# A 256-token decoder layer on one core: the LRU's gates as fp32r halves, its softplus moved, its input in four banks, and memory's sums moved

## The chip, the cores and the metric

The kernel runs on one core of a Trainium2 chip. The metric is the device time of one execution in microseconds; the figure for the kernel before is the median of three runs. Engines are named as the profile names them: PE (TensorE; PEld is its weight load), DVE (VectorE), ACT (ScalarE), POOL (GpSimd) and SP (SyncE, which issues most DMAs).

## What is computed

One layer of an autoregressive decoder on 256 tokens of width 2048, in float32. The normalised input goes through one projection `w_in` whose columns are split among three groups of heads; the part that the change touches is the first group, the RG-LRU (512 channels, four diagonal blocks of 128), and the normalisations.

```python
h = rms_norm(x, mix_norm_g)
p = h @ w_in                       # split: lru_x, lru_z, ml_u, ml_o, ml_z, ml_i, ml_f, mo_q, mo_k, mo_v, mo_z
# group A, RG-LRU
xc = causal_conv(lru_x, conv_w, conv_b)              # four taps
r = sigmoid(block_diag(xc, wa) + ba)
i = sigmoid(block_diag(xc, wx) + bx)
log_a = -8.0 * r * softplus(-lam)
a = exp(log_a)
u = sqrt(-expm1(2.0 * log_a)) * (i * xc)
h_t = a_t * h_(t-1) + u_t
y_lru = h * silu(lru_z)
# group B: mLSTM on ml_*; group C: block attention on mo_*
x = x + concat(y_lru, y_ml, y_mo) @ w_out
# cross-attention into 256 memory tokens
x = x + memory_cross_attention(rms_norm(x, xa_norm_g), rms_norm(mem, mem_norm_g), xa_wq, xa_wkv, xa_wo)
out = rms_norm(x, final_norm_g)
```

## The kernel before

**Chunks.** All weight matrices are cut on the host into one stream `ws` of 512 KB chunks (some are smaller) in the order of the table `GROUPS`: lx (the LRU's input, 8 chunks), u0, u2, u4 (4 each), lz0 (4), o0 and o1 (8 each), lz2, q, k, z, v, out0 to out3, and then the cross-attention's. A chunk is loaded to a tile `raw` (4 buffers), copied by ACT to `wh`, its value rounded to fp32r, and DVE writes the remainder `wl` = raw - wh (6 buffers of each; `split`, lines 182 to 211: the copy is line 204, the subtraction goes through the helper `tt` of line 150). The activations are split in the same way (`a_x`, with the high and the low half side by side). A product is then three fp32r products: high by high, high by low, low by high.

**Matmuls.** `mm` issues the matmuls of a chunk. Groups of kind "C" (weights stationary, lines 267 and 268) use one 512-wide matmul for high by (high, low) and one 256-wide for low by high; their accumulators are two PSUM banks, one for each 128 columns, and whoever takes them out adds the two halves of the bank (`add_halves`, line 466). Kind "W", which only lx has, uses three 256-wide matmuls into half a bank (lines 274 to 281), so four blocks of columns fit two banks and need no addition. Kind "X" has the activations stationary (lines 289 to 291). Accumulators come from a pool of 4 banks, all other PSUM tiles from a second pool of 4 (`ps`).

**The order.** The program's order is the order of issue: every engine takes its instructions in order. The main loop goes over the chunks i. In each turn it splits up to chunk i + 4, issues the matmuls of chunk i, and lets `step` advance one piece of the background queue `bg` by one `yield`. When the last chunk of a group is done, `done` appends the work that has become possible.

**The LRU.** When lx is done, `lru_evac` copies it out; `stats("x")` (line 429) turns the sums of squares of x into the root mean square of each token (`rstd_x` on DVE and POOL), forms diagonal matrices `d_x` of it (line 447) and, two turns later, multiplies them by ones on PE (line 453), so that each token's factor stands in a row in all partitions (`rrow`); `lru_scale` multiplies on POOL. `softplus_lam` (line 389) works on 128 x 4 numbers in a chain of small DVE instructions and one Exp on ACT. `lru_core` runs the convolution, block by block: ACT the first tap, DVE three multiply-adds (line 510), one block in a turn; then the gates, two blocks in a turn: two fp32 matmuls with the weights `lw` and two sigmoids on ACT for each block (lines 516 to 519); then exponentials, the square root and the scan.

```python
bg(idle(2), stats("x"), lru_scale(), u_scale(), call(softplus_lam), lru_core())
```

**Memory.** While PE works on out2 and out3, `mem_stats` loads the memory, squares it on ACT, sums on POOL, and `stats("m")` sums over the partitions on PE (line 438), forms `d_m` and multiplies it on PE (line 453). It stands in the queue behind the four loads of x for the residual (`x1_load`), each of which takes a turn.

Of the kernel before, what the change touches and what calls it, by code (L numbers as in the profile page):

```python
# [39 lines left out]
def _t(off, *tiles):  # L40
# [4 lines left out]
    ("lx", "w_in", "W", "x", _cols(*_t(O_LX, 0, 1, 2, 3))),  # L45
# [61 lines left out]
def kernel(ctx: ExitStack, tc: tile.TileContext, xT, memT, x, mem, ws, vec_d, lw_d, fg_d, out):  # L107
# [144 lines left out]
    def mm(i):  # L252
# [3 lines left out]
        if j == 0:  # L256
            acc[g] = [accp.tile([128, 512], F32, tag="acc", name=f"acc_{name}{b}") for b in range(2)]
        a = acc[g]
        for kk in range(kc):
# [3 lines left out]
            if kind == "C":  # L263
                both = act_all[act][k // 2][:, k % 2, :, :].rearrange("p a b -> p (a b)")
                for m in range(2):
                    sl = slice(kk * n + m * 128, kk * n + m * 128 + 128)
                    P.matmul(a[m], h[:, sl], both, start=first, stop=False, skip_group_check=True)  # L267
                    P.matmul(a[m][:, :256], l[:, sl], xh, start=False, stop=last, skip_group_check=True)  # L268
            elif kind == "W":
                mv_h, mv_l = xh, xl  # L270
                for m in range(n // 128):
                    o = a[m // 2][:, (m % 2) * 256:(m % 2) * 256 + 256]
                    sl = slice(kk * n + m * 128, kk * n + m * 128 + 128)
                    P.matmul(o, h[:, sl], mv_h, start=first and m % 2 == 0, stop=False, skip_group_check=True)
                    P.matmul(o, h[:, sl], mv_l, start=False, stop=False, skip_group_check=True)
                    if i:
                        P.matmul(o, l[:, sl], mv_h, start=False, stop=last, skip_group_check=True)
                for m in range(n // 128 if i == 0 else 0):
                    o = a[m // 2][:, (m % 2) * 256:(m % 2) * 256 + 256]
                    sl = slice(kk * n + m * 128, kk * n + m * 128 + 128)  # L280
                    P.matmul(o, l[:, sl], mv_h, start=False, stop=False, skip_group_check=True)
# [57 lines left out]
    def expand(name, blk):  # L339
        t = bdp.tile([128, 6, 128], F32, name=f"bd_{name}", tag="bd")  # L340
        bd[name] = t
        for c in range(6):
            G.tensor_tensor(t[:, c, :].rearrange("p (b o) -> p b o", o=4), dmask,
                            blk(c)[:, None, :].to_broadcast([128, 32, 4]), OP.mult)

# [83 lines left out]
    def stats(which):  # L429
# [19 lines left out]
        if which == "x":  # L449
            yield  # L450
# [39 lines left out]
    def lru_evac(a):  # L490
# [3 lines left out]
        for b in range(2):  # L494
            S.activation(xp[:, 2 * b:2 * b + 2, 3:259], bank(a, b), AF.Copy)
# [8 lines left out]

    def lru_core():
        xp = L["xp"]
        xc = big(2, 4, 256)
        for c in range(4):
# [775 lines left out]
```

## Time and profile before

| | |
|---|---|
| runs | 518.6, 518.79, 519.13 us (median 518.79) |
| the profiled execution | 518.12 us, of which its span is 516.4 us |
| PE busy | 506.7 us (98%) |
| DVE busy | 345.4 us (67%) |
| ACT busy | 301.2 us (58%) |
| POOL busy | 60.3 us (12%) |
| HBM | 190 GB/s over the span |

The span runs from the program's first instruction to its last; the remaining 1.7 us of the profiled execution lie around it. Times in rows are counted from the span's start. An instruction's duration reaches from its start to its modelled end; on PE and, less so, on ACT and DVE the next instruction starts before that, so a cost is best read from the difference of two starts. "[idle before <-X]" is how long the engine sat idle before the row, and what ended that.

### The profile page before, as it was taken

To read this page: it belongs to the slowest core of one execution; us is meant where nothing else is said; L and a number is where in the kernel's file an instruction comes from. 1 tells how busy PE (TensorE), PEld (TensorE's weight loads), DVE (VectorE), ACT (ScalarE), POOL (GpSimd) and SP (SyncE) were. 2 spreads that over 40 slices of the span, in tenths; PEclk is the share of its full clock that TensorE was granted. 3 is DMA by queue.
4 is the path that set the end of the run, shared out by engine and by line. 5 is a ranking of instruction groups with operands and counts; after the bars stand their busy time and mean duration, and the time that the engine had idled before them with its cause. 6 is when DMAs were issued, how large, how long until landed. Compare 5 with 4: busy or idle time off the path is not lost.

```text
span 516.4 us, 7502 instructions
## 1 busy us (share of the span) xinstructions
PE 506.7 (98%) x2746; PEld 444.1 (86%) x2746; DVE 345.4 (67%) x558; ACT 301.2 (58%) x498; POOL 60.3 (12%) x76
## 2 busy tenths in 40 slices
PE   9999999999999999999999999999999999999994
PEld 7998889988888888889988888888888788888883
DVE  6758955797478755747745567654767857748774
ACT  6685677679563533353545756544558567748444
POOL 1804112000151111002000000000141111000000
PEclk9999999999999999999999999999999999999997
DMA  8996454567645545436743365578594555643704
GB/s 293 400 343 238 133 163 128 154 204 235 214 148 168 174 164 163 149 96 212 241 160 124 130 205 175 183 251 324 191 332 124 190 176 165 197 169 96 265 7 162
DMA packets 31508, 98.73 MB, mean 191 GB/s; under 512 B 3568, under 2 KB 4720, under 8 KB 31472
## 3 DMA queue, kind: packets, MB, share of 16 engines
q1 hardware_dynamic: 30896, 97.59, 56.6%
q10 hardware_dynamic: 576, 0.66, 0.4%
q8 instruction: 21, 0.34, 0.3%
q14 instruction: 15, 0.12, 0.1%
HBM read 96.15 MB, written 2.10 MB: 190 GB/s over the span
## 4 chain that ended last, share of the span: by engine, by line
PE 86%; DVE 4%; ACT 3%; issue 2%; DMA 2%; POOL 1%; SPq 0%; ACTq 0%; DVEq 0%; POOLq 0%
PE acc_out L291 5%; PE acc_out L289 5%; PE acc_out L290 5%; PE acc_u L267 4%; PE acc_k L267 4%; PE acc_q L267 4%; PE acc_z L291 4%; PE acc_z L289 4%; PE acc_z L290 4%; PE acc_cq L267 3%; PE acc_ck L267 3%; PE acc_q L268 2%; PE acc_u L268 2%; PE acc_k L268 2%; PE acc_v L291 2%
## 5 line engine op out<-in xcount | busy, mean ns | idle before, releaser
L150 DVE TENSOR_TENSOR wl<-raw,wh 128x1024 fp32r<-128x1024 f32 (+4 forms) x169 | 199.8, 1197 | 95.6 <-ACT wh L204 93.2
L204 ACT ACTIVATE wh<-raw 128x1024 fp32r<-128x1024 f32 (+2 forms) x160 | 158.8, 1013 | 35.7 <-DMA raw<-ws 12.3
L289 PE MATMUL acc_out<-wh,a_y 128*128 128x512 f32 x128 | 50.8, 397 | 0.0
L291 PE MATMUL acc_out<-wh,a_y 128*128 128x512 f32 x128 | 50.0, 390 | 0.0
L290 PE MATMUL acc_out<-wl,a_y 128*128 128x512 f32 x128 | 49.8, 389 | 0.0
L289 PE MATMUL acc_z<-wh,a_x 128*128 128x512 f32 x96 | 39.6, 413 | 0.0
L291 PE MATMUL acc_z<-wh,a_x 128*128 128x512 f32 x96 | 37.6, 392 | 0.0
L290 PE MATMUL acc_z<-wl,a_x 128*128 128x512 f32 x96 | 37.5, 390 | 0.0
L267 PE MATMUL acc_k<-a_x,wh 128*128 128x512 f32 x96 | 34.4, 402 | 0.0
L267 PE MATMUL acc_q<-a_x,wh 128*128 128x512 f32 x96 | 34.3, 399 | 0.0
L267 PE MATMUL acc_u<-a_x,wh 128*128 128x512 f32 x96 | 34.0, 399 | 0.0
L474 POOL TENSOR_TENSOR w<-ev,rrow 128x512 f32<-128x512 f32 x10 | 16.9, 1691 | 133.3 <-DVE ev L150 120.5
L291 PEld LDWEIGHTS acc_out<-wh,a_y 128*128 128x128 f32 x128 | 24.0, 188 | 5.1
L290 PEld LDWEIGHTS acc_out<-wl,a_y 128*128 128x128 f32 x128 | 24.1, 188 | 4.7
L289 PEld LDWEIGHTS acc_out<-wh,a_y 128*128 128x128 f32 x128 | 24.0, 188 | 4.6
L268 PE MATMUL acc_u<-a_x,wl 128*128 128x256 f32 x96 | 27.0, 281 | 0.0
L268 PE MATMUL acc_q<-a_x,wl 128*128 128x256 f32 x96 | 26.9, 280 | 0.0
L268 PE MATMUL acc_k<-a_x,wl 128*128 128x256 f32 x96 | 26.8, 279 | 0.0
L414 POOL TENSOR_TENSOR mask<-mask,yt 128x512 f32<-128x512 f32 x7 | 9.8, 1397 | 145.8 <-ACT yt L413 145.8
L267 PE MATMUL acc_lz<-a_x,wh 128*128 128x512 f32 x64 | 23.4, 406 | 0.0
L267 PE MATMUL acc_ck<-a_m,wh 128*128 128x512 f32 x64 | 22.9, 401 | 0.0
L267 PE MATMUL acc_cq<-a_h,wh 128*128 128x512 f32 x64 | 22.7, 399 | 0.0
(325 smaller groups left out, 1171.8 us busy)
## 6 DMA issues: line engine op xcount, KB each, us to landing
raw<-ws SPq DMA_DIRECT2D x138, 512.0 KB, 3.7
raw<-ws SPq DMA_DIRECT2D x24, 384.0 KB, 3.1
w<-x SPq DMA_DIRECT2D x8, 512.0 KB, 6.3
raw<-ws SPq DMA_DIRECT2D x8, 392.0 KB, 3.3
w<-memT SPq DMA_DIRECT2D x8, 256.0 KB, 3.7
w<-xT SPq DMA_DIRECT2D x7, 256.0 KB, 5.2
out<-xg SPq DMA_DIRECT2D x5, 256.0 KB, 2.9
w<-fg SPq DMA_DIRECT2D x2, 512.0 KB, 5.6
```

Source lines behind the costliest of these rows:

```text
L150: V.tensor_tensor(out, a, b, op)
L204: S.activation(h[:, :kc * n], r[:, :kc * n], AF.Copy)
L267: P.matmul(a[m], h[:, sl], both, start=first, stop=False, skip_group_check=True)
L268: P.matmul(a[m][:, :256], l[:, sl], xh, start=False, stop=last, skip_group_check=True)
L289: P.matmul(o, xh[:, sl], mh, start=first, stop=False)
L290: P.matmul(o, xh[:, sl], ml, start=False, stop=False)
L291: P.matmul(o, xl[:, sl], mh, start=False, stop=last)
L414: G.tensor_tensor(sq[which], sq[which], q, OP.add)
L474: G.tensor_tensor(dst, e, rb(which), OP.mult)
```

## The change

1. lx becomes a group of kind "C": four PSUM banks, one for each block of 128 columns, all of the accumulators' pool; u0, the next group, takes two banks of the other pool. `lru_evac` adds the two halves of each bank, as other groups do. For chunk 0 the low matmuls still stand behind all high ones.
2. The gates' matmuls work on fp32r halves: `lw_halves` splits the gates' weights (after chunk 11), `lru_core` splits each block of the convolution's result (ACT copies, DVE subtracts), and each gate takes three fp32r matmuls for one fp32. The four new tiles come from the activations' pool.
3. `softplus_lam` leaves the queue and is issued in turn 9 of the main loop, before that turn's square of x.
4. The four loads of x take two turns for four, `mem_stats` waits one turn more behind its last square, and `stats("m")` leaves two turns between its diagonal matrices and their matmuls, as `stats("x")` does.

```diff
@@ -42,7 +42,7 @@
 
 
 GROUPS = [
-    ("lx", "w_in", "W", "x", _cols(*_t(O_LX, 0, 1, 2, 3))),
+    ("lx", "w_in", "C", "x", _cols(*_t(O_LX, 0, 1, 2, 3))),
     ("u0", "w_in", "C", "x", _cols(*_t(O_U, 0, 1))),
     ("u2", "w_in", "C", "x", _cols(*_t(O_U, 2, 3))),
     ("u4", "w_in", "C", "x", _cols(*_t(O_U, 4, 5))),
@@ -254,7 +254,12 @@
         name, mat, kind, act, cols = GROUPS[g]
         h, l = hi_w.pop(i), lo_w.pop(i)
         if j == 0:
-            acc[g] = [accp.tile([128, 512], F32, tag="acc", name=f"acc_{name}{b}") for b in range(2)]
+
+            if name == "u0":
+                acc[g] = [ps(), ps()]
+            else:
+                acc[g] = [accp.tile([128, 512], F32, tag="acc", name=f"acc_{name}{b}")
+                          for b in range(4 if name == "lx" else 2)]
         a = acc[g]
         for kk in range(kc):
             k = kc * j + kk
@@ -262,23 +267,21 @@
             first, last = k == 0, k == NK - 1
             if kind == "C":
                 both = act_all[act][k // 2][:, k % 2, :, :].rearrange("p a b -> p (a b)")
-                for m in range(2):
-                    sl = slice(kk * n + m * 128, kk * n + m * 128 + 128)
-                    P.matmul(a[m], h[:, sl], both, start=first, stop=False, skip_group_check=True)
-                    P.matmul(a[m][:, :256], l[:, sl], xh, start=False, stop=last, skip_group_check=True)
-            elif kind == "W":
-                mv_h, mv_l = xh, xl
+
+                def high(m):
+                    P.matmul(a[m], h[:, kk * n + m * 128:kk * n + m * 128 + 128], both, start=first, stop=False,
+                             skip_group_check=True)
+
+                def low(m):
+                    P.matmul(a[m][:, :256], l[:, kk * n + m * 128:kk * n + m * 128 + 128], xh, start=False, stop=last,
+                             skip_group_check=True)
+
                 for m in range(n // 128):
-                    o = a[m // 2][:, (m % 2) * 256:(m % 2) * 256 + 256]
-                    sl = slice(kk * n + m * 128, kk * n + m * 128 + 128)
-                    P.matmul(o, h[:, sl], mv_h, start=first and m % 2 == 0, stop=False, skip_group_check=True)
-                    P.matmul(o, h[:, sl], mv_l, start=False, stop=False, skip_group_check=True)
+                    high(m)
                     if i:
-                        P.matmul(o, l[:, sl], mv_h, start=False, stop=last, skip_group_check=True)
-                for m in range(n // 128 if i == 0 else 0):
-                    o = a[m // 2][:, (m % 2) * 256:(m % 2) * 256 + 256]
-                    sl = slice(kk * n + m * 128, kk * n + m * 128 + 128)
-                    P.matmul(o, l[:, sl], mv_h, start=False, stop=False, skip_group_check=True)
+                        low(m)
+                for m in range(0 if i else n // 128):
+                    low(m)
             else:
                 mh, ml = h[:, kk * n:kk * n + n], l[:, kk * n:kk * n + n]
                 for t in range(2):
@@ -342,6 +345,10 @@
         for c in range(6):
             G.tensor_tensor(t[:, c, :].rearrange("p (b o) -> p b o", o=4), dmask,
                             blk(c)[:, None, :].to_broadcast([128, 32, 4]), OP.mult)
+
+    def halves_tile(name):
+
+        return acts.tile([128, 2, 2, 256], F32R, tag="y", name=name)
 
     def late_consts():
         G.memset(dmask, 1.0)
@@ -446,8 +453,7 @@
             for t in range(2):
                 V.tensor_scalar(d[:, i, t, :], ident, rr[:, t:t + 1], None, op0=OP.mult)
         yield
-        if which == "x":
-            yield
+        yield
         p = ps()
         for i in range(2):
             P.matmul(p[:, :256], ones_r, d[:, i].rearrange("p a b -> p (a b)"), start=i == 0, stop=i == 1)
@@ -491,8 +497,9 @@
         xp = big(1, 4, 259)
         L["xp"] = xp
         V.memset(xp[:, :, 0:3], 0.0)
-        for b in range(2):
-            S.activation(xp[:, 2 * b:2 * b + 2, 3:259], bank(a, b), AF.Copy)
+        for m in range(4):
+            S.activation(xp[:, m, 3:259], a[m][:, 256:], AF.Copy)
+            tt(xp[:, m, 3:259], a[m][:, :256], xp[:, m, 3:259], OP.add)
         yield
 
     def lru_scale():
@@ -502,19 +509,35 @@
             G.tensor_tensor(v, v, rb("x"), OP.mult)
         yield
 
+    def lw_halves():
+        h, l = (halves_tile(n).rearrange("p a b c -> p (a b c)").rearrange("p (a b) -> p a b", a=8)
+                for n in ("lw_h", "lw_l"))
+        S.activation(h, lw, AF.Copy)
+        tt(l, lw, h.bitcast(F32), OP.subtract)
+        L["lw"] = h, l
+
     def lru_core():
         xp = L["xp"]
         xc = big(2, 4, 256)
+        lwh, lwl = L["lw"]
+        xs = [halves_tile(f"xc{j}") for j in range(2)]
         for c in range(4):
             S.activation(xc[:, c, :], xp[:, c, 0:256], AF.Identity, scale=vc("cw", 4 * c), bias=vc("cb", c))
             for j in range(1, 4):
                 stt(xc[:, c, :], xp[:, c, j:j + 256], vc("cw", 4 * c + j), xc[:, c, :], OP.mult, OP.add)
+            h, l = (xs[c // 2][:, c % 2, i, :] for i in range(2))
+            S.activation(h, xc[:, c, :], AF.Copy)
+            tt(l, xc[:, c, :], h.bitcast(F32), OP.subtract)
             yield
         r, ig = big(3, 4, 256), big(4, 4, 256)
         for c in range(4):
             p = ps()
-            P.matmul(p[:, :256], lw[:, c, :], xc[:, c, :], start=True, stop=True)
-            P.matmul(p[:, 256:], lw[:, 4 + c, :], xc[:, c, :], start=True, stop=True)
+            h, l = (xs[c // 2][:, c % 2, i, :] for i in range(2))
+            for i in range(2):
+                o, k = p[:, 256 * i:256 * i + 256], 4 * i + c
+                P.matmul(o, lwh[:, k, :], h, start=i == 0, stop=False, skip_group_check=True)
+                P.matmul(o, lwh[:, k, :], l, start=False, stop=False, skip_group_check=True)
+                P.matmul(o, lwl[:, k, :], h, start=False, stop=True, skip_group_check=True)
             S.activation(r[:, c, :], p[:, :256], AF.Sigmoid, bias=vc("ba", c))
             S.activation(ig[:, c, :], p[:, 256:], AF.Sigmoid, bias=vc("bx", c))
             if c % 2:
@@ -884,10 +907,11 @@
     XT_TAGS = (3, 4, 7, 8)
     ssq1 = small("ssq1", 2, 4)
 
-    def x1_load(g):
-        X1[g] = big(XT_TAGS[g], 2, 512)
-        nc.sync.dma_start(X1[g], bass.AP(tensor=x.tensor, offset=x.offset + g * 512,
-                                         ap=[[D, 128], [128 * D, 2], [1, 512]]))
+    def x1_load(*groups):
+        for g in groups:
+            X1[g] = big(XT_TAGS[g], 2, 512)
+            nc.sync.dma_start(X1[g], bass.AP(tensor=x.tensor, offset=x.offset + g * 512,
+                                             ap=[[D, 128], [128 * D, 2], [1, 512]]))
         yield
 
     def x1_evac(a, g):
@@ -1113,7 +1137,7 @@
             if j >= 2:
                 square("m", j - 2)
             yield
-        yield
+        yield from idle(2)
         yield from stats("m")
 
     def call(f, *args):
@@ -1124,7 +1148,7 @@
     def done(name, a):
         if name == "lx":
             urgent(lru_evac(a))
-            bg(idle(2), stats("x"), lru_scale(), u_scale(), call(softplus_lam), lru_core())
+            bg(idle(2), stats("x"), lru_scale(), u_scale(), lru_core())
         elif name == "u0":
             u_sum(a)
         elif name == "u2":
@@ -1160,7 +1184,7 @@
             bg(ml_y(), mo_y(0, 1))
         elif name == "z2":
             urgent(gate_z(name, a))
-            bg(mo_y(1, 3), x1_load(0), x1_load(1), x1_load(2), x1_load(3), mem_stats())
+            bg(mo_y(1, 3), x1_load(0, 1), x1_load(2, 3), mem_stats())
         elif name.startswith("out"):
             g = int(name[3])
             urgent(x1_evac(a, g))
@@ -1203,6 +1227,10 @@
             xrow_load(i - 2)
         if i == 6:
             nc.sync.dma_start(lw, lw_d)
+        if i == 9:
+            softplus_lam()
+        if i == 11:
+            lw_halves()
         if 6 <= i < 10:
             xrow_square(i - 6)
         g, j, kc = CHUNKS[i][:3]
```

In the built program's order, DVE between the splits of chunk 13 and of chunk 19, with the statistics of x (rstd_x, d_x), the softplus (sp_e to nsp8) and the convolution's first block (w2). Before:

```order
L150 TENSOR_TENSOR wl13_527<-raw13_432,wh13_526 128x1024
L150 TENSOR_TENSOR wl14_550<-raw14_438,wh14_549 128x1024
L433 TENSOR_REDUCE rstd_x_571<-ssqx_129 128x2
L447 TENSOR_SCALAR d_x_579<-ident_118,rl_576 128x128 x2
L150 TENSOR_TENSOR wl15_585<-raw15_470,wh15_584 128x1024
L150 TENSOR_TENSOR wl18_668<-raw18_553,wh18_667 128x1024
L153 SCALAR_TENSOR_TENSOR sp_e_689<-vec_90 128x4
L398 TENSOR_SCALAR nsp8_128<-sp8_127 128x4
L153 SCALAR_TENSOR_TENSOR w2_713<-w1_497,vec_90,w2_713 128x256 x3
L150 TENSOR_TENSOR wl19_719<-raw19_588,wh19_718 128x1024
```

And now, with lw_l and xc0, the low halves of the gates' weights and of the block:

```order
L150 TENSOR_TENSOR wl13_471<-raw13_386,wh13_470 128x1024
L153 SCALAR_TENSOR_TENSOR sp_e_492<-vec_90 128x4
L405 TENSOR_SCALAR nsp8_128<-sp8_127 128x4
L150 TENSOR_TENSOR wl14_518<-raw14_392,wh14_517 128x1024
L440 TENSOR_REDUCE rstd_x_539<-ssqx_129 128x2
L454 TENSOR_SCALAR d_x_547<-ident_118,rl_544 128x128 x2
L150 TENSOR_TENSOR wl15_553<-raw15_416,wh15_552 128x1024
L150 TENSOR_TENSOR lw_l_575<-w9_123,lw_h_574 128x1024
L150 TENSOR_TENSOR wl18_640<-raw18_521,wh18_639 128x1024
L153 SCALAR_TENSOR_TENSOR w2_661<-w1_435,vec_90,w2_661 128x256 x3
L150 TENSOR_TENSOR xc0_662<-w2_661,xc0_662 128x256
L150 TENSOR_TENSOR wl19_671<-raw19_556,wh19_670 128x1024
```

The softplus has moved from behind wl18 to behind wl13, ahead of wl14 and of the statistics; lw_l stands behind wl15, and a subtraction behind each block's multiply-adds.

ACT over two blocks of the convolution (the first taps write w2; wh21 and wh22 are the next chunks' high halves). Before:

```order
L509 ACTIVATE w2_713<-w1_497,vec_90 128x256
L204 ACTIVATE wh21_774<-raw21_648 128x1024
L509 ACTIVATE w2_713<-w1_497,vec_90 128x256
L204 ACTIVATE wh22_800<-raw22_671 128x1024
L509 ACTIVATE w2_713<-w1_497,vec_90 128x256
```

And now:

```order
L529 ACTIVATE xc0_662<-w2_661 128x256
L204 ACTIVATE wh21_728<-raw21_620 128x1024
L525 ACTIVATE w2_661<-w1_435,vec_90 128x256
L529 ACTIVATE xc1_663<-w2_661 128x256
L204 ACTIVATE wh22_756<-raw22_643 128x1024
L525 ACTIVATE w2_661<-w1_435,vec_90 128x256
L529 ACTIVATE xc1_663<-w2_661 128x256
```

A copy of the block to its high half stands between each first tap and the next chunk's wh.

PE around memory's sums, in out3 (chunks 136 to 139). Before:

```order
L291 MATMUL acc_out31_3742<-wh137_3768,a_y5_3228 128x512
L438 MATMUL ps58_3899<-ones_109,mask_3519 128x1 x2
L289 MATMUL acc_out30_3741<-wh138_3799,a_y6_3274 128x512
L291 MATMUL acc_out31_3742<-wh138_3799,a_y6_3274 128x512
L453 MATMUL ps59_3936<-d_m_3908,ones_r_111 128x256 x2
L289 MATMUL acc_out30_3741<-wh139_3825,a_y7_3300 128x512
```

And now:

```order
L294 MATMUL acc_out31_3723<-wh136_3716,a_y4_3132 128x512
L445 MATMUL ps60_3850<-ones_109,mask_3457 128x1 x2
L292 MATMUL acc_out30_3722<-wh137_3749,a_y5_3202 128x512
L294 MATMUL acc_out31_3723<-wh138_3780,a_y6_3248 128x512
L459 MATMUL ps61_3910<-d_m_3859,ones_r_111 128x256 x2
L292 MATMUL acc_out30_3722<-wh139_3803,a_y7_3274 128x512
```

The sums stand behind chunk 136 for 137; the matmuls on d_m stay behind chunk 138.

## Rows read from the trace of the kernel before

**Rows 1.** The page: part 1, and the granted clock of part 2 (tenths, 40 slices).
```profile
PE 506.7 (98%) x2746; PEld 444.1 (86%) x2746; DVE 345.4 (67%) x558; ACT 301.2 (58%) x498; POOL 60.3 (12%) x76
PEclk9999999999999999999999999999999999999997
```

**Rows 2.** Timeline of PE, chunk 40: start, duration, engine, line, operation, out<-in, shape.
```profile
112.28 0.40 PE L267 MATMUL acc_lz<-a_x,wh 128*128 128x512 f32 x1
112.81 0.39 PE L268 MATMUL acc_lz<-a_x,wl 128*128 128x256 f32 x1
```

**Rows 3.** Timeline of PE, the first matmuls of chunks 2 and 3 of lx.
```profile
11.85 0.28 PE L274 MATMUL acc_lx<-a_x,wh 128*128 128x256 f32 x1
...
14.73 0.28 PE L274 MATMUL acc_lx<-a_x,wh 128*128 128x256 f32 x1
```

**Rows 4.** Timeline of PE: the matmuls on d_x, and chunk 13 to chunk 14's start.
```profile
43.26 0.40 PE L453 MATMUL ps<-d_x,ones_r 128*128 128x256 f32 x2
43.50 0.40 PE L267 MATMUL acc_u<-a_x,wh 128*128 128x512 f32 x1
...
46.32 0.40 PE L267 MATMUL acc_u<-a_x,wh 128*128 128x512 f32 x1
```

**Rows 5.** Timeline of ACT: two copies from u0's accumulators, and wh19.
```profile
40.34 0.69 ACT L466 ACTIVATE ev<-acc_u 128x256 f32<-128x256 f32 x2
...
51.52 1.05 ACT L204 ACTIVATE wh<-raw 128x1024 fp32r<-128x1024 f32 x1
```

**Rows 6.** Timeline of PE: gates of blocks 0 and 1, of blocks 2 and 3.
```profile
66.11 0.59 PE L516 MATMUL ps<-w,w 128*128 128x256 f32 x2
66.54 0.59 PE L517 MATMUL ps<-w,w 128*128 128x256 f32 x2
...
70.62 0.59 PE L516 MATMUL ps<-w,w 128*128 128x256 f32 x2
```

**Rows 7.** Timeline of DVE: wl12 to wl18, softplus, first and last convolution block, wl23.
```profile
35.44 1.23 DVE L150 TENSOR_TENSOR wl<-raw,wh 128x1024 fp32r<-128x1024 f32 x1 [2.18 <-ACT wh L204]
37.42 1.23 DVE L150 TENSOR_TENSOR wl<-raw,wh 128x1024 fp32r<-128x1024 f32 x1 [0.76 <-ACT wh L204]
39.41 1.23 DVE L150 TENSOR_TENSOR wl<-raw,wh 128x1024 fp32r<-128x1024 f32 x1 [0.76 <-ACT wh L204]
...
42.80 1.22 DVE L150 TENSOR_TENSOR wl<-raw,wh 128x1024 fp32r<-128x1024 f32 x1
...
44.61 6.20 DVE L150 TENSOR_TENSOR wl<-raw,wh 128x1024 fp32r<-128x1024 f32 x3
50.73 0.15 DVE L153 SCALAR_TENSOR_TENSOR sp_e<-vec 128x4 f32<-128x4 f32 x1
...
54.30 1.52 DVE L153 SCALAR_TENSOR_TENSOR w<-w,vec,w 128x256 f32<-128x256 f32 x3
...
64.85 1.52 DVE L153 SCALAR_TENSOR_TENSOR w<-w,vec,w 128x256 f32<-128x256 f32 x3
66.29 1.22 DVE L150 TENSOR_TENSOR wl<-raw,wh 128x1024 fp32r<-128x1024 f32 x1
```

**Rows 8.** Timeline of ACT: the gates' table load, first sigmoids of either turn, wh26.
```profile
64.64 1.28 ACT L518 ACT_TABLE_LOAD   x1
67.18 0.47 ACT L518 ACTIVATE w<-ps,vec 128x256 f32<-128x256 f32 x1 [1.26 <-PE ps L517]
...
71.68 0.47 ACT L518 ACTIVATE w<-ps,vec 128x256 f32<-128x256 f32 x1 [2.05 <-PE ps L517]
...
73.27 0.85 ACT L204 ACTIVATE wh<-raw 128x784 fp32r<-128x784 f32 x1
```

**Rows 9.** Timeline of PE: end of chunk 138, matmuls on d_m, chunk 139.
```profile
406.26 0.39 PE L291 MATMUL acc_out<-wh,a_y 128*128 128x512 f32 x1
407.34 0.69 PE L453 MATMUL ps<-d_m,ones_r 128*128 128x256 f32 x2 [0.69 <-DVE d_m L447]
407.87 0.40 PE L289 MATMUL acc_out<-wh,a_y 128*128 128x512 f32 x1
```

## The prediction

> **What bounds the kernel now.** I read the page first: PE is busy for 506.7 of 516.4 us and its clock row holds 9 until the last slice [rows 1]. So time is lost or won only where PE gets less to do, or waits. Second, PE's timeline: matmuls follow each other without a gap nearly everywhere, so a term on PE is a difference of starts, and the reader is to look at starts, since a row's duration overlaps the next. Third, how far DVE and ACT, which split each weight chunk into halves, are ahead of PE. I number chunks as the tiles raw, wh, wl are numbered (lx is 0 to 7, u 8 to 19, lz0 20 to 23, o0 and o1 24 to 39, lz2 from 40). The lead is several us at the convolution, and nothing at chunk 40: there PE starts a high matmul at 112.28 and its low one only at 112.81, where 0.24 would do [rows 2]. Whatever makes DVE or ACT later between the LRU's gates and this point moves the end by as much.
>
> **The change, part by part.**
>
> Lx in four banks. Now a chunk of lx takes 14.73 - 11.85 = 2.88 us for 24 matmuls [rows 3]; a chunk in the form that lx gets takes 46.32 - 43.50 = 2.82 [rows 4]. PE gains 0.06 to 0.09 in each of chunks 1 to 7: 0.5 us. Evacuating four banks takes ACT four copies of 256 columns for two of 512; two such copies take 0.69 [rows 5], so ACT is some 0.3 us later afterwards. The four adds fall into idle time of DVE (it sat idle 2.18 us before wl12 [rows 7]).
>
> Gates in halves. An fp32 gate matmul goes every 66.54 - 66.11 = 0.43 us for its two passes [rows 6]: 8 of them 3.46. The 24 that replace them, at the 0.12 of lx (2.88 for 24), take 2.88. PE gains 0.6.
>
> Softplus moved. Its 19 small DVE instructions run from 50.73 to 54.30, 3.57 us, between wl18 and the convolution [rows 7]. They go in behind wl13, ahead of wl14 and of the RMS statistics of x. DVE leaves wl13 at 38.65, with ACT's 0.3 at 38.9; DVE is in order, so earlier idle time is of no use. Softplus ends at 42.45, wl14 starts there and not at 39.41: 3.04 later. All that follows on DVE up to d_x comes 3.04 later: d_x is complete where wl15 starts behind it, at 42.80 and now at 45.84. PE wants it at 43.26 [rows 4] less the 0.5 of lx, about 42.75. It had 0.4 us to spare; now PE stands for about 3.2 us with the restart, net of lx 2.7 later than before. Nothing hides this: the matmul on d_x stands in PE's order ahead of chunk 13.
>
> The halves of the gates' weights (lw_l, one more 1024-wide subtraction) follow wl15: 1.15. From wl15's start at 45.84 come wl15 1.16, lw_l 1.15, the two adds 0.65, wl16 to wl18. These three took 6.1 us from 44.61 to 50.73, since GpSimd scaled beside them [rows 7]; it does so again, as its row waits for the same d_x. The sum is 45.84 + 9.1 = 54.9 for the start of the convolution, against 54.30: the softplus that left has been spent.
>
> The convolution in ping-pong. Now a block is three multiply-adds and one wl: 66.29 - 64.85 = 1.44 and 1.14, or 2.6 us, with ACT's half of the next chunk ready in advance. Afterwards ACT copies each block to xc's high half when its third multiply-add ends, DVE subtracts, and ACT's next wh stands behind that copy. A block is then: multiply-adds 1.52, hand-over and copy; the wh starts 0.3 after the copy does and takes 1.05 [rows 5]; wl 1.14 behind it. That is 1.57 + 1.41 + 1.14 = 4.1 us, and DVE's subtraction lies inside ACT's wh. No row shows this copy; it lies between half of the 0.69 of two copies of its size from the accumulators and half of the 1.05 of one four times as wide, 0.35 to 0.53, and since the wh is pipelined behind it, the two ends move a block by 0.1 either way. I take 0.42, the middle. Four blocks cost 4 x 1.55 = 6.2 more. wl23 starts at 66.29 + 0.6 + 6.2 = 73.1, and its wh on ACT at 72.0.
>
> From there ACT goes on without a wait (copies less the 0.1 by which the next one starts early): wh23 0.95, two copies 0.59 [rows 5], wh24 0.75, the table load 1.28, four sigmoids 73.27 - 71.68 = 1.59, wh25 0.75, four sigmoids 1.59 [rows 8]. That is 7.5: wh26 starts at 79.5 instead of 73.27, 6.2 later. Before, ACT had waited 1.26 and 2.05 us for PE's gates on this way [rows 8]; that spare time is used up and more. PE, 2.7 late and 0.6 better in the gates, is only 2.1 later and reaches the gates of blocks 2 and 3 (before: 70.62 [rows 6]) at about 73.1, with xc complete at 72.5: barely no wait.
>
> From wh26 to chunk 40 each step of the LRU hands over between ACT, DVE and GpSimd and none waits for PE, so all of it stays 6.2 later, while PE is 2.1 later. The lead shrinks by 4.1, PE runs dry from about chunk 30 on, in pieces near 1 us, and passes chunk 40 when wl40 comes: **6.2 us later than before**. The 0.5, the 0.6 and most of the 3.2 us wait lie inside this; they are not added. Bounds: with a third less of GpSimd's hold-up around wl16 to wl18 (0.85) and with the cheap copy (0.4), 4.9; with lw_l drawn out like its neighbours (2.0 instead of 1.15) and the dear copy, 7.4.
>
> Memory's sums. PE now goes from 406.26 to 407.34 where 0.23 would do, and its two statistics matmuls take 407.87 - 407.34 = 0.53 where 0.24 would do [rows 9]: 1.14 us. The sums come one chunk (2.7 us) sooner and the matmuls stay where they are, so what now ends 0.69 too late ends some 2 us early: **-1.1**. The x loads that share a step go to tiles long free, and PE waits for no wl in this stage: the splits' lead hides the squares' new place, two chunks earlier.
>
> Sum: +6.2 - 1.1 = **+5.1**. On the profiled execution, 518.12 us, that is 523.2; its run lies 0.67 below the median of the three, 518.79, so I predict **523.9**, own range 522.6 to 525.1.
>
> [...]
>
> **The rivals.**
> [...]
> *Only PE's wait counts.* If the convolution is 3.4 us shorter than I sum it, ACT is again waiting for PE at the second sigmoids, chunk 40 moves by PE's 2.1 alone, and with -1.1 the result is 519.8. For it: ACT now has 3.3 us of waits there [rows 8]. Against it: the four hand-overs alone cost 6.2.
> *Faster.* If DVE comes to the softplus earlier than wl13's end allows (38.65) by 3 us, so that d_x is there by 42.75, and a hand-over costs under 0.3 us, PE keeps its gains: -0.5 - 0.6 - 1.1 = -2.2, 516.6. Against it: wl13 waited 0.76 for ACT [rows 7], which worked on without a gap.
> *Memory's wait stays*, since another DVE item takes the place: 523.9 + 1.1 = 525.0.
>
> **How the numbers follow.** The forecast gets 0.70, the clock 0.05, only PE's wait 0.12, faster 0.10, memory's wait 0.03. The predicted time is the forecast's, 523.9. The range must also take in 519.8 with its own blur, so it is 519.6 to 526.0; left out are the faster case and half of the clock's. A measurement of this kernel can tell about 0.2% (1.0 us) from no change, which is 517.8 to 519.8: half of the 519.8 case falls inside. Faster 0.10, same 0.06, slower 0.84.
>
> **What would show it.** Right: a PE wait of about 3 us on d_x ahead of chunk 13; ACT's xc copies each waiting for DVE, wl19 to wl23 some 4 us apart; no ACT wait for PE at the second sigmoids; several PE waits on wl between chunks 30 and 40, 4 to 6 us together; no wait on d_m. Wrong: ACT still waiting for PE at the sigmoids, or no wait on d_x; if the convolution's blocks stay near 2.6 us apart, the largest term falls.

## The result, and the profile after

| | before | with the change |
|---|---|---|
| median | 518.69 us (4 runs, 518.55 to 519.13) | 523.19 us (4 runs, 522.85 to 523.85) |
| the profiled execution | 518.12 us, span 516.4 | 522.85 us, span 520.8 |

The ratio is 1.0094, 95% interval 1.0082 to 1.0106: **slower by 4.5 us**. The forecast was 523.9, 5.1 us slower.

The chain of causes starts at d_x. PE's waits in the changed kernel, engine and line first, then what it waited for; total, times, longest in us:

```profile
PE ps L459 <- DVE d_x L454: 2.4, 1, 2.4
PE acc_o L293 <- DVE wl L150: 2.1, 4, 0.7
PE acc_lx L272 <- ACT wh L193: 0.8, 1, 0.8
```

The wait on d_m is gone, one on d_x of 2.4 us is new, and PE now waits for low halves in o0 and o1. The wait of 0.8 us in lx's first chunk does not stand in every execution: here ACT waited 1.41 us for a load of weights, and the second profile of the same kernel (below) has no such wait of PE. The last matmul of lx, before and with the change:

```profile
29.01 0.28 PE L277 MATMUL acc_lx<-a_x,wl 128*128 128x256 f32 x1
```

```profile
28.68 0.28 PE L276 MATMUL acc_lx<-a_x,wl 128*128 128x256 f32 x1
```

ACT's waits between 30 and 85 us:

```profile
ACT xc L529 <- DVE w L153: 14.4, 4, 6.4
ACT rrow L462 <- PE ps L459: 1.8, 1, 1.8
ACT sp_e L400 <- DVE sp_e L153: 1.4, 1, 1.4
```

The waits for PE's gates (1.26 and 2.05 us, [rows 8]) have left this list; in their place ACT waits 14.4 us for the convolution. PE's timeline around d_x, against [rows 4]:

```profile
42.80 0.28 PE L276 MATMUL acc_u<-a_x,wl 128*128 128x256 f32 x1
45.44 0.78 PE L459 MATMUL ps<-d_x,ones_r 128*128 128x256 f32 x2 [2.36 <-DVE d_x L454]
46.06 0.39 PE L272 MATMUL acc_u<-a_x,wh 128*128 128x512 f32 x1
```

Chunk 13 starts at 46.06 where it started at 43.50, 2.56 later. DVE's timeline, against [rows 7]: the softplus ahead of wl14, wl14, wl15 and the halves of the gates' weights; then wl16 to wl18 and the blocks of the convolution.

```profile
38.70 0.16 DVE L153 SCALAR_TENSOR_TENSOR sp_e<-vec 128x4 f32<-128x4 f32 x1
...
42.30 1.23 DVE L150 TENSOR_TENSOR wl<-raw,wh 128x1024 fp32r<-128x1024 f32 x1
...
45.70 1.22 DVE L150 TENSOR_TENSOR wl<-raw,wh 128x1024 fp32r<-128x1024 f32 x1
46.83 1.22 DVE L150 TENSOR_TENSOR lw_l<-w,lw_h 128x1024 fp32r<-128x1024 f32 x1
...
48.64 5.91 DVE L150 TENSOR_TENSOR wl<-raw,wh 128x1024 fp32r<-128x1024 f32 x3
54.48 1.51 DVE L153 SCALAR_TENSOR_TENSOR w<-w,vec,w 128x256 f32<-128x256 f32 x3
...
65.50 1.52 DVE L153 SCALAR_TENSOR_TENSOR w<-w,vec,w 128x256 f32<-128x256 f32 x3
67.50 0.42 DVE L150 TENSOR_TENSOR xc<-w,xc 128x256 fp32r<-128x256 f32 x1 [0.49 <-ACT xc L529]
68.45 1.23 DVE L150 TENSOR_TENSOR wl<-raw,wh 128x1024 fp32r<-128x1024 f32 x1 [0.52 <-ACT wh L204]
69.59 1.52 DVE L153 SCALAR_TENSOR_TENSOR w<-w,vec,w 128x256 f32<-128x256 f32 x3
...
72.55 1.23 DVE L150 TENSOR_TENSOR wl<-raw,wh 128x1024 fp32r<-128x1024 f32 x1 [0.53 <-ACT wh L204]
```

wl16 to wl18 took 5.91 us together, where wl15 took 1.22. GpSimd scaled beside them, as it did before (6.20 us, [rows 7]), and lw_l, at 46.83 beside the first of its rows, took 1.22 all the same. These rows, before and with the change:

```profile
44.16 3.34 POOL L502 TENSOR_TENSOR w<-w,rrow 128x512 f32<-128x512 f32 x2 [2.46 <-ACT rrow L456]
47.45 2.27 POOL L574 TENSOR_TENSOR w<-ev,rrow 128x512 f32<-128x512 f32 x1
```

```profile
46.72 4.52 POOL L509 TENSOR_TENSOR w<-w,rrow 128x512 f32<-128x512 f32 x2 [2.12 <-ACT rrow L462]
51.20 2.27 POOL L597 TENSOR_TENSOR w<-ev,rrow 128x512 f32<-128x512 f32 x1
```

The block from 65.50 to 69.59 is the whole mechanism in four rows: 4.09 us, in which DVE waits twice, 0.49 us for ACT's copy and 0.52 us for the wh behind it, and subtracts for 0.42 us in between. Before, a block was 1.44 + 1.14 us with no wait in it. ACT's side, against [rows 8]: the copies of blocks 2 and 3, the table load, and wh26.

```profile
67.05 0.42 ACT L529 ACTIVATE xc<-w 128x256 fp32r<-128x256 f32 x1 [2.23 <-DVE w L153]
67.38 1.04 ACT L204 ACTIVATE wh<-raw 128x1024 fp32r<-128x1024 f32 x1
...
71.15 0.42 ACT L529 ACTIVATE xc<-w 128x256 fp32r<-128x256 f32 x1 [2.24 <-DVE w L153]
71.47 1.04 ACT L204 ACTIVATE wh<-raw 128x1024 fp32r<-128x1024 f32 x1
...
73.83 1.28 ACT L541 ACT_TABLE_LOAD   x1
75.12 0.47 ACT L541 ACTIVATE w<-ps,vec 128x256 f32<-128x256 f32 x1
...
78.74 0.91 ACT L204 ACTIVATE wh<-raw 128x784 fp32r<-128x784 f32 x1
```

ACT runs without a wait from the last copy to wh26, which starts at 78.74 in place of 73.27: 5.47 later. PE's timeline at chunk 33, at chunk 40 (against [rows 2]) and at memory's statistics (against [rows 9]):

```profile
99.69 0.44 PE L292 MATMUL acc_o<-wh,a_x 128*128 128x384 f32 x1
100.68 0.44 PE L293 MATMUL acc_o<-wl,a_x 128*128 128x384 f32 x1 [0.55 <-DVE wl L150]
...
118.37 0.39 PE L276 MATMUL acc_lz<-a_x,wl 128*128 128x256 f32 x1
...
411.83 0.39 PE L294 MATMUL acc_out<-wh,a_y 128*128 128x512 f32 x1
412.06 0.40 PE L459 MATMUL ps<-d_m,ones_r 128*128 128x256 f32 x2
412.29 0.39 PE L292 MATMUL acc_out<-wh,a_y 128*128 128x512 f32 x1
```

At chunk 33 the low matmul comes 0.99 us behind the high one. Such holes stand at chunks 30, 33, 35 and 36; by starts, those from chunk 30 to 40 make 4.4 us together, of which the kernel before has 1.0 too, at chunks 37 to 40. The low matmul of chunk 40 starts at 118.37 against 112.81: **5.56 later**. At memory's statistics PE goes from 411.83 to 412.29, 0.46 us for what took 407.87 - 406.26 = 1.61: **1.15 less**. The two make 4.4, the difference of the spans; another 0.3 lies outside the span.

### The profile page after: what moved, and what is told of

The parts are those of the page before. It is cut to its first block, busy times and chain, and to the rows that moved or that the text cites. A ratio compares the mean times of both kernels' runs of the same rounds, so it can differ in the third digit from the quotient of the medians.

```text
span 520.8 us, 7407 instructions
## 1 busy us (share of the span) xinstructions
PE 506.6 (97%) x2690; PEld 439.7 (84%) x2690; DVE 348.6 (67%) x567; ACT 303.3 (58%) x505; POOL 64.4 (12%) x76
## 4 chain that ended last, share of the span: by engine, by line
PE 78%; DVE 8%; ACT 6%; DMA 4%; issue 3%; POOL 1%; SPq 0%; ACTq 0%; DVEq 0%; POOLq 0%
PE acc_out L292 6%; PE acc_out L294 6%; PE acc_out L293 6%; PE acc_k L272 4%; PE acc_q L272 4%; PE acc_z L294 4%; PE acc_z L292 4%; PE acc_z L293 4%; DMA raw<-ws 4%; DVE wl L150 3%; PE acc_cq L272 3%; PE acc_ck L272 3%; ACT wh L204 3%; PE acc_q L276 2%; PE acc_k L276 2%
## 5 line engine op out<-in xcount | busy, mean ns | idle before, releaser
L293 PE MATMUL acc_o<-wl,a_x 128*128 128x392 f32 (+1 forms) x64 | 22.4, 350 | 2.1 <-DVE wl L150 2.1
L272 PE MATMUL acc_lx<-a_x,wh 128*128 128x512 f32 x64 | 22.5, 402 | 0.9 <-ACT wh L193 0.8
L272 PE MATMUL acc_u<-a_x,wh 128*128 128x512 f32 x64 | 22.7, 399 | 0.0
```

The costliest lines, as they stand in the source:

```text
L272: P.matmul(a[m], h[:, kk * n + m * 128:kk * n + m * 128 + 128], both, start=first, stop=False, skip_group_check=True)
L293: P.matmul(o, xh[:, sl], ml, start=False, stop=False)
```

## The experiments

Two explanations were open. One is the prediction's: ACT and DVE hand each block of the convolution back and forth, the LRU's chain comes late, and PE runs dry at chunks 30 to 40. The other: PE's 2.4 us on d_x, which nothing hides, are the larger part of what is paid. The kernel before was measured again beside each group of runs. Expectations reckon from its median beside an earlier group (518.7 with the result, 518.2 beside the first four runs), so what an expectation got right is read from the difference to the kernel before in the run's own group, which each result names.

**The softplus alone put back.**

```diff
-            bg(idle(2), stats("x"), lru_scale(), u_scale(), lru_core())
+            bg(idle(2), stats("x"), lru_scale(), u_scale(), call(softplus_lam), lru_core())
...
-        if i == 9:
-            softplus_lam()
```

> The whole change, but the softplus of lambda stands where it stood before, ahead of the convolution. Theory (the LRU's chain through ACT and DVE sets the time, not PE's wait on d_x): PE's 2.4 us wait on d_x is gone and chunk 13 starts near 43.2, but the convolution's first multiply-add comes near 55.7 (softplus 3.6 us ahead of it, d_x 3.0 us sooner), wh26 some 1.2 us later than with the change, PE waits longer for wl between chunks 30 and 40, and the result is no better: about 524.4 (523.2 with the change). Rival (the wait on d_x is what the change pays with): the 2.4 us come back, about 520.6.

Measured: 524.43 us against 518.18, ratio to before 1.0113 (1.0093 to 1.0132). PE's wait on d_x was gone and chunk 13 started at 43.75, yet the kernel was no faster than with the change: its first multiply-add came at 55.73, 1.25 later, and wh26 at 80.00, 1.26 later. The rival falls: the wait on d_x costs the change nothing, since PE would only wait longer later. Its waits, and chunk 40's low matmul:

```profile
PE acc_o L293 <- DVE wl L150: 2.4, 4, 0.7
PE ps L538 <- ACT xc L529: 1.4, 1, 1.4
```

```profile
119.64 0.39 PE L276 MATMUL acc_lz<-a_x,wl 128*128 128x256 f32 x1
```

**The gates back in fp32.** The 24 matmuls become 8 in fp32, and no halves are made.

```diff
-            S.activation(h, xc[:, c, :], AF.Copy)
-            tt(l, xc[:, c, :], h.bitcast(F32), OP.subtract)
...
-        if i == 11:
-            lw_halves()
```

> The whole change without the halves of the gates: the four blocks are fp32 matmuls as before, no halves of their weights; the softplus stays ahead of wl14, lx and memory's sums as changed. Theory (hand-overs of the ping-pong between DVE and ACT are the cost): PE still waits 2.4 us on d_x, but blocks of the convolution take 2.6 us again, ACT waits for PE at the sigmoids again, and only PE's 2.6 us reach chunk 40: about 520.1 (before 518.7 + 2.6 - 1.2). Rival (the softplus ahead of d_x is the whole cost, the halves cost nothing): about 523.2.

Measured: 520.89 us against 518.18, ratio 1.0043 (1.0028 to 1.0058), some 2 us under the change. The blocks took 61.62 - 59.05 = 2.57 us, and ACT waited for PE at the sigmoids again. DVE's starts of two blocks:

```profile
59.05 1.51 DVE L153 SCALAR_TENSOR_TENSOR w<-w,vec,w 128x256 f32<-128x256 f32 x3
...
61.62 1.52 DVE L153 SCALAR_TENSOR_TENSOR w<-w,vec,w 128x256 f32<-128x256 f32 x3
```

It came out 2.7 above the kernel before, where the expectation's sum was 2.6 - 1.2 = 1.4: 1.3 more, for a reason that this run was the first to show. Behind the wait on d_x the granted clock fell, to 0.50 of full speed between 46 and 48 us. Windows of PE, its busy time, the granted clock as a share of full speed, DMA share and GB/s:

```profile
40.00:42.00 2.00, 2.00 (x13) 1.00 0.64 227
42.00:45.00 3.00, 1.00 (x6) 1.00 0.26 78
45.00:49.00 4.00, 3.81 (x13) 0.57 0.53 182
49.00:55.00 6.00, 6.00 (x37) 1.00 0.68 223
```

PE had stood still for 2.2 us; chunk 13 then took 4.07 us (45.97 to 50.04) in place of 2.82. These 1.25 us are what the expectation lacked.

**Lx in four banks and memory's sums alone.** Both edits above together.

> Only lx in four banks and memory's sums; softplus and fp32 gates as before. Theory: PE gains 0.34 in lx and 1.16 at memory's statistics, no wait on d_x, no long wait on wl beyond the kernel before's: about 517.2. Rival (the four evacuations and adds of lx make ACT and DVE late and cost what is lost at chunks 30 to 40): 518.7 or more.

Measured: 516.74 us against 518.18, ratio 0.9963 (0.9947 to 0.9978): 1.4 us faster, as expected. These two parts are gains.

**The split a step later.** The copy and the subtraction are issued at the start of the next step, behind the wh.

```diff
-            S.activation(h, xc[:, c, :], AF.Copy)
-            tt(l, xc[:, c, :], h.bitcast(F32), OP.subtract)
...
             yield
+            halve(c)
```

`halve(c)` holds the two removed lines.

> The whole change, but ACT's copy and DVE's subtraction for a block's halves are issued one step later, so that ACT has the next wh behind it before it needs the block. Theory (the cost of the halves is the wait of ACT's queue for the multiply-adds, not the added work): ACT's 14.4 us of waits for the convolution go, blocks fall from 4.1 us to about 2.9, wh26 comes 3 to 4 us sooner, and what is left is PE's wait on d_x: about 519.5. Rival (the work itself, four copies and four subtractions and 24 matmuls, is the cost): within 0.5 us of the change's 523.2.

Measured: 521.70 us against 518.18, ratio 1.0055 (1.0037 to 1.0073). The mechanism went as expected: blocks of 66.62 - 63.72 = 2.90 us, ACT's waits for the convolution down from 14.4 to 3.5 us, PE's gates awaited again, wh26 at 77.37. The size was a miss by 2.7 (3.5 above the kernel before, 0.8 expected): with ACT no longer late, PE's own losses count, and they were larger. Its wait on d_x was 3.5 us in this execution, and the clock fell behind it, to 0.50 between 48 and 50 us: chunk 13 took 4.36 us in place of 2.82. PE was 4.2 us late at o0's start (82.09 against 77.89) and still 4.2 late at chunk 40's low matmul (116.97 against 112.81), so nothing but its own lateness was left.

**The softplus alone moved, in the kernel before.**

```diff
-            bg(idle(2), stats("x"), lru_scale(), u_scale(), call(softplus_lam), lru_core())
+            bg(idle(2), stats("x"), lru_scale(), u_scale(), lru_core())
...
+        if i == 9:
+            softplus_lam()
```

> The kernel before with one edit: the softplus of lambda goes to where the change puts it, ahead of wl14 and of d_x. Theory (d_x is late, and PE stands for it with nothing behind): PE waits some 2.5 us ahead of chunk 13, and since ACT waits for PE at the sigmoids all later steps shift with it: +2.5, about 520.7 against 518.2, if the granted clock stays at 2.4 GHz behind the wait; if it falls to 1.2 GHz for a little over one chunk, as it did in the runs with fp32 gates and with the split a step later, +3.8, about 522.0. Rival (the DVE queue ahead of the convolution is relieved and the lead grows): 518.2 or less.

Measured: 522.75 us against 518.66, ratio 1.0074 (1.0055 to 1.0094), six runs from 520.11 to 524.46. In the profiled one PE waited 2.0 us on d_x, the clock was 0.57 between 45 and 49 us, and chunk 13 took 4.00. The run of 520.11 had the highest mean clock of the six, 0.996, the others 0.991 to 0.994. (The traces give the clock as a share of full speed alone: the two levels that this expectation, like that of the first repair below, names in GHz are 1.00 and 0.50 there, and GHz are shown by no run.) So this part alone costs some 4 us in the kernel before: its lateness and the clock both reach the end, since nothing else is late.

**The change once more.**

> The change itself once more, for the clock behind PE's wait on d_x. [...] Theory (the time is set by the LRU's chain, which covers what PE loses there): 523.2 whether it falls or not; if it falls in the profile, chunk 40 stays where it was, near 118.4. Rival (PE's place counts): a run in which the clock falls is 1.3 us longer, near 524.5.

Measured: 522.54 us against 518.50, ratio 1.0076 (1.0064 to 1.0088), five runs from 522.44 to 522.92. With fp32 gates, the split a step later and the softplus alone, the clock had fallen behind waits of 2.2, 3.5 and 2.0 us; this time it fell in the change too, behind a wait of 2.4 us, as long as in the first profile:

```profile
40.00:42.00 2.00, 2.00 (x14) 1.00 0.47 174
42.00:45.00 3.00, 0.64 (x5) 0.92 0.37 112
45.00:49.00 4.00, 4.00 (x16) 0.63 0.53 182
49.00:55.00 6.00, 6.00 (x36) 1.00 0.58 180
```

Chunk 13 took 3.84 us, 1.0 more, and chunk 40's low matmul came at 117.79, no later than with the clock up (118.37):

```profile
117.79 0.39 PE L276 MATMUL acc_lz<-a_x,wl 128*128 128x256 f32 x1
```

This execution was ahead from the start, since lx had no wait in its first chunk: its last matmul started at 28.34 against 28.68, and the first multiply-add at 53.88 against 54.48. From that multiply-add to chunk 40's low matmul it is 63.91 us here and 63.89 there, although PE came to o0 at 80.21, 0.18 later than in the first profile (80.03). The theory holds: ACT's chain covers what PE loses at d_x, at either clock.

**The copy on DVE.** One word of the softplus-back kernel changes: the engine that copies a block.

```diff
-            S.activation(h, xc[:, c, :], AF.Copy)
+            V.tensor_copy(h, xc[:, c, :])
```

> The whole change, the softplus in its old place, and a block's copy to its high half on DVE in place of ACT: the same work, but no hand-over to ACT in the convolution. Theory (the hand-overs DVE, ACT, DVE are the cost of the halves, not their work): blocks of about 3.3 us in place of 4.1, block 3's halves done near 68, ahead of GpSimd's scaling beside which a subtraction of 128x256 took 1.50 in place of 0.42 us and held PE for 1.6 us in the run with the split a step later; PE keeps lx, gates and memory: 518.7 - 0.3 - 0.6 - 1.2 = 516.5, and 0.3 more outside the span, as in every kernel with halved gates so far: 516.9. Rival (DVE is the bound of the convolution, whoever copies): PE waits for xc or wl again, 518.3 or more.

Measured: 516.30 us against 518.50, ratio 0.9960 (0.9946 to 0.9974), where the kernel with the copy on ACT had 524.43 against 518.18: **8 us for the engine of four copies**. DVE has more work and is done sooner:

```profile
64.44 1.52 DVE L153 SCALAR_TENSOR_TENSOR w<-w,vec,w 128x256 f32<-128x256 f32 x3
66.00 0.29 DVE L529 CAST xc<-w 128x256 fp32r<-128x256 f32 x1
66.33 0.42 DVE L150 TENSOR_TENSOR xc<-w,xc 128x256 fp32r<-128x256 f32 x1
66.67 1.22 DVE L150 TENSOR_TENSOR wl<-raw,wh 128x1024 fp32r<-128x1024 f32 x1
67.80 1.52 DVE L153 SCALAR_TENSOR_TENSOR w<-w,vec,w 128x256 f32<-128x256 f32 x3
```

A block is 67.80 - 64.44 = 3.36 us without a wait, and ACT is far ahead with its wh (wh23 at 61.79, wl23 at 70.03). Nothing else differs between the two kernels, and chunk 40's low matmul came at 111.72 in place of 119.64, so the hand-over is shown to be the cost of the halves.

**Where the room is at chunks 37 to 40.** To the kernel with lx and memory alone, all four blocks of fp32 gates in one step:

```diff
-            if c % 2:
+            if c == 3:
                 yield
```

> Lx in four banks and memory's sums, softplus and fp32 gates as before, and all four blocks of the gates in one step in place of two. Theory (what the LRU's chain is late for is chunks 37 to 40): the chain comes a step sooner, the waits on wl at chunks 37 to 40 (1.0 us in the kernel before) go, about 515.8, 1.0 under the run with lx and memory alone. Rival (these waits come from the splits' own pace, not from the LRU's steps): 516.7.

Measured: 515.54 us against 518.66, ratio 0.9948 (0.9936 to 0.9960), the fastest median of all: 3.1 under the kernel before, where lx and memory alone were 1.4 under it. The waits at chunks 37 to 40, which the kernel before has too (1.0 us by starts), were gone in its profile. The lateness that PE meets there comes from the LRU's steps. The profiled execution, 517.38, is the slowest of the five; in it PE waited 1.7 us in lx's first chunk, and its last lx matmul started at 29.55, where the other profiles with lx in four banks have 28.3 to 29.0.

**Three repairs that gave less than they should.** First, the whole change with two edits from above, `halve(c)` behind the `yield` and `call(softplus_lam)` back in the queue.

> The whole change with two repairs: the softplus stands where it stood before, and a block's halves are issued a step later. Theory (the change's two costs are the order on DVE ahead of d_x and the hand-overs of the convolution, not the halves as such): no wait on d_x, the granted clock stays at 2.4 GHz, blocks of 2.9 us, ACT waits for PE at the second sigmoids; all three gains are kept (0.3 in lx, 0.6 in the gates, 1.2 at memory): about 516.1. Rival (lw_l and the softplus together make the convolution so late that ACT no longer waits for PE, and chunk 40 sees it): 517.5 or more.

Measured: 518.36 us against 518.66, 0.9994 (0.9985 to 1.0003): 0.3 under the kernel before, where 2.1 were expected. Of the 1.8 that lack, 0.3 lie outside the span, and 1.4 are a wait of PE for block 3's low half, since DVE's subtraction took 1.50 us where block 2's in the same run took 0.42. PE's row, and the two engines' rows, of that run:

```profile
72.90 0.39 PE L543 MATMUL ps<-xc,lw_h 128*128 128x256 f32 x1 [1.40 <-DVE xc L150]
```

```profile
71.34 1.50 DVE L150 TENSOR_TENSOR xc<-w,xc 128x256 fp32r<-128x256 f32 x1
```

```profile
70.63 1.93 POOL L480 TENSOR_TENSOR w<-ev,rrow 128x512 f32<-128x512 f32 x1 [9.42 <-DVE ev L150]
```

The subtraction began while GpSimd scaled and ended 0.3 us behind it. Block 0's, which began at 59.98 beside a GpSimd row of 59.01 to 61.21, took 1.51 us; block 1's, with none beside it, took 0.42. That GpSimd holds the subtraction up is read from these rows alone; how it does so is not shown. (It is this run that the expectation of the copy on DVE means by its hold-up of PE.)

Second, the same with the gates in one step and the softplus split in two: its first DVE step and Exp at chunk 9, the rest behind the convolution.

```diff
+        softplus_rest(*L["sp"])
         r, ig = big(3, 4, 256), big(4, 4, 256)
...
-            softplus_lam()
+            L["sp"] = softplus_lam()
```

> The whole change with three repairs: a block's halves issued a step later; of the softplus only its first DVE step and its Exp stand early, its other steps behind the convolution, where DVE was idle; all four blocks of the gates in one step. Theory: all gains of the run before this, and the waits of 1.0 us at chunks 37 to 40 go too: about 515.2. Rival (the gains do not add, since the chain's lead at chunk 40 is set by other steps): 516.1.

Measured: 518.35 us against 518.66, 0.9998 (0.9989 to 1.0007), a miss by some 3. ACT's early Exp waited 1.4 us for DVE and held wh14 back, so d_x came late (PE waited 1.3 us), and PE waited 0.7 us for block 3.

Third, the copy on DVE, the gates in one step, and the same cut of the softplus with its Exp in the old place.

```diff
+        softplus_rest(*L["sp"])
...
-            bg(idle(2), stats("x"), lru_scale(), u_scale(), call(softplus_lam), lru_core())
+            bg(idle(2), stats("x"), lru_scale(), u_scale(), call(softplus_exp), lru_core())
```

> The kernel with the copy on DVE and the softplus's first step and Exp in the old place, its other steps behind the convolution, and all four blocks of the gates in one step. Theory: no wait on d_x, none on xc, and none on wl at chunks 37 to 40: 1.0 under the run with the copy on DVE, about 515.9 (515.5 in the run with the gates in one step and no halves). Rival (DVE's four copies and subtractions make block 3 late for gates that come a step sooner): PE waits for xc, 516.9 or more.

Measured: 518.82 us against 518.50, 1.0008 (0.9998 to 1.0018), a miss by 3 again. The softplus's end now came behind wl24, and ACT's table load ahead of the LRU's first Exp waited 4.5 us for it. PE had hardly a wait at the gates (0.2 us), and ran dry at chunks 32 to 40 all the same. It is the same chain, broken at another link.

**The softplus spread over DVE's gaps.** The copy on DVE, the gates in one step, and the softplus in four pieces behind chunks 4 to 7.

```diff
...
-        if i == 9:
-            softplus_lam()
+        if 4 <= i < 8:
+            next(sp_steps, None)
...
```

> The change's parts put where their engines have room: a block's copy on DVE, the softplus in four pieces spread over the steps of chunks 4 to 7 (DVE sat idle 1.1 to 1.3 us ahead of each of wl9 to wl11), all four blocks of the gates in one step. Theory: the pieces cost nothing, the convolution starts 3.6 us sooner than in the run with the copy on DVE, block 3's halves are done when PE comes to them, no waits on d_x and none on wl at chunks 37 to 40: 1.0 under that run, about 515.3. Rival (the pieces make wl9 to wl13 and so d_x late, or PE comes to the gates before block 3): a PE wait there, 516.3 or more.

Measured: 516.62 us against 518.50, 0.9965 (0.9953 to 0.9977), six runs from 515.63 to 517.57. Its profile (the run of 515.63) has what was expected: PE's timeline at chunk 40, with no gap between high and low.

```profile
111.17 0.39 PE L272 MATMUL acc_lz<-a_x,wh 128*128 128x512 f32 x1
111.40 0.28 PE L276 MATMUL acc_lz<-a_x,wl 128*128 128x256 f32 x1
```

The median is 1.3 above the expectation, and why its runs spread over 2 us was not found. A candidate is the wait in lx's first chunk, which was 0.3 us in this profile and 1.7 in that of the gates in one step; that the other runs had it is not shown. By their intervals this kernel, the copy on DVE alone, the gates in one step, and lx with memory alone cannot be put in order; all four are faster than both kernels of this case.

## Why the prediction was right

- **Lx**: forecast 0.5, measured 0.33: the last lx matmul started at 28.68 in place of 29.01. But PE had waited 0.83 us for chunk 0's weights in that execution; in the second profile, without this wait, it started at 28.34, 0.67 sooner than before. So the size was about right, and one execution does not tell it closer.
- **d_x**: PE 2.7 later forecast, 2.56 measured. 3.2 was forecast for the wait with the restart; the wait was 2.4, and the matmuls on d_x took 46.06 - 45.44 = 0.62 in place of 0.24. wl14 started at 42.30, forecast 42.45. The step held; that this wait does not count was in the sum and is shown by the softplus-back run and by the change once more.
- **Start of the convolution**: forecast 54.9, measured 54.48. The softplus's room was spent as said; wl16 to wl18 took 5.91 beside GpSimd, 6.1 was forecast.
- **Blocks**: forecast 4.1 us, measured 4.09; the copy taken as 0.42 measured 0.42. wl23 forecast at 73.1, came at 72.55.
- **Gates**: forecast 0.6. PE was 2.57 late at lz0's start (65.85 against 63.28) and 2.14 at o0's, so 0.43 came back; it was forecast to be 2.1 late there.
- **wh26**: forecast 6.2 later, measured 5.47. Of the 0.7 too much, 0.4 is the convolution's start; and 0.3 the two groups of four sigmoids, which took 1.44 and 1.43 (78.74 - 77.31) in place of 1.59 each.
- **Chunk 40**: forecast 6.2 later, measured 5.56, inside its bounds of 4.9 to 7.4. PE ran dry from chunk 30 on, and the holes of 4.4 us together are within the 4 to 6 named as a sign.
- **Memory**: forecast -1.1, measured -1.15.
- **Left out**: the 0.3 us outside the span (below). 5.56 - 1.15 + 0.3 = 4.7 is the profiled execution's difference, 522.85 - 518.12; the forecast had 5.1. That the total is so near is in part luck: the 0.6 too much at chunk 40 and the 0.3 left out have opposite signs.
- **Clock**: 0.05 in the chances, for a lower clock behind PE's wait on d_x. The clock of the kernel before falls only in its last slice [rows 1], and PE does not wait on d_x there, so it was the author's guess; the range leaves half of this case out, above 526.0, and no run shows such a time: the change's nine runs lie between 522.44 and 523.85. What the runs show is a fall: of the five kernels in which PE waits over 1 us on d_x, the clock fell behind the wait in the profiles of four: fp32 gates (wait 2.2, clock 0.57 between 45 and 49 us), split later (3.5, 0.79), softplus alone (2.0, 0.57), and the change on its second profile (2.4, 0.63). The fifth, the second of the three repairs, waited 1.3 us. The first profile of the change, with the same wait of 2.4 us and a clock of 1.00, does not show it. Chunk 13 lost 1.0 to 1.5 us by it (3.84 to 4.36 in place of 2.82), and in the change none of that reached chunk 40. The chance was for the outcome, and that was rightly small; its place is a kernel that is bound by PE there, as in the run with the softplus alone.
- **Only PE's wait counts** fell with the softplus-back run. (Its 3.4 us follow from the sum: ACT at the second four sigmoids at 79.5 - 1.59 = 77.9, PE through the gates at 73.1 + 12 x 0.12 = 74.5.) It named the right condition: where the convolution is shorter (fp32 gates, split later), PE's lateness is what remains.
- **Faster** and **Memory's wait stays** fell with the profile: d_x came late, a hand-over cost some 0.5 us (0.49 and 0.52 in the block above), and the wait on d_m was gone.

## What to carry to other kernels

Ahead of splitting work between two in-order engines, count hand-overs, not busy time: a block that goes DVE, ACT, DVE with ACT's next work queued behind it cost 1.5 us per block, and the same copy on DVE itself, 0.29 us of added work, cost the kernel 8 us less. PE's wait of 2.4 us on d_x cost this change nothing, since a later stage was later still: without it, the softplus put back, the kernel was 6.2 us above the kernel before, with it 4.5 and 4.0. So the removal of a wait is to be priced at the next place where that engine runs dry. And a step put "where the engine idles" has to be followed to every queue that it stands in: twice here an Exp or its input held the other engine (1.4 us ahead of wh14, 4.5 us ahead of the LRU's first Exp).

## What had not been expected of the hardware

- The time outside the span is 2.0 to 2.1 us in every run of the five kernels in which ACT copies the blocks (the change, softplus back, split later, and the first two repairs), and 1.7 to 1.8 in every run of the others, halved gates with the copy on DVE included. What happens there no trace shows.
- PE's wait in the first chunk of lx's new form differs from profile to profile, from none to 1.7 us, and the last matmul of lx starts between 28.3 and 29.55. A term of half a microsecond in lx cannot be read from one profile.
- The same wait of 2.4 us on d_x was followed by a granted clock of 1.00 in one profile of the change and by 0.63 between 45 and 49 us in the other, and waits of 2.0, 2.2 and 3.5 us in other kernels by a fall each time (0.57, 0.57 and 0.79 in the same window). What decides it stays open.
